# Experts' counts on TensorE: one load of 6 or 9 registers for two or three pairs, without assertions

## The chip, the cores and the metric

The kernel runs on one core of one Trainium2 chip. The metric is the device time of one execution in microseconds (us), the median of several runs.

## The reference

Two layers of a transformer over 256 latent tokens and 256 context tokens of width 1024. Each layer has a mixer (linear attention beside grouped attention in layer 0, a state-space scan beside Fourier mixing in layer 1) and a mixture of 16 experts. What the change touches is the experts:

```python
s = jax.nn.sigmoid((h @ router_w).astype(F32))
sel = (s + router_b).reshape(n, N_EXPERT_GROUPS, EXPERTS_PER_GROUP)
g_idx = jnp.argmax(lax.top_k(sel, TOP_K)[0].sum(-1), axis=-1)      # one group for each token
_, loc = lax.top_k(in_group, TOP_K)                                # two experts of it
...
return (jax.nn.silu(xb @ w_gate[ei]) * (xb @ w_up[ei])) @ w_down[ei]   # d_expert 768
```

Each token goes to two of the 16 experts and gets the weighted sum of their outputs. Layer 0 routes all 512 tokens, layer 1 the 256 latent ones. So each expert sees a number of tokens that is known at run time only: its count.

## The kernel before, in words

A program written with a planner: the source traces instructions in an order, and the planner orders each engine's queue by dependences, buffers and its own costs, unless an edge fixes it. Matrix products are fp32, with 32 tokens at a time in the array (128x32 weights load, 384 or 256 columns of expert weights streamed).

`experts` handles one layer. The 16 experts go in eight pairs (p, with m = 0 or 1 in it). For each pair `lists` builds from the routing positions which tokens go to it: VectorE writes a one-hot matrix `G` (tile G0p in layer 0, which has a single buffer), and TensorE multiplies it with a small table (`entries`, tile sl0p or sl1p, four matmuls for each half of a pair). In layer 0 the lists of pairs 0 and 1 are made ahead and in expert 0, and those of the last six pairs in one call, traced at the end of expert 1's iteration. GpSimd then gathers the pair's rows from DRAM (`gather`), TensorE transposes them (`features`, tile xt0p), `hidden` runs gate and up (tiles gu0p, gu1p; a part of 32 tokens at a time, over four weight chunks) and `down` the second product (dp0p, dp1p) one expert later. Results go back by a scatter (first pairs of layer 0) or by one-hot products (`combine`, cm0p, cm1p).

Parts of 32 tokens that may be empty stand in conditional blocks (`when`): TensorE compares a register with a constant and branches; where the expert has no such tokens, one short matmul with zeros fills the tile (the rows with `<-zero`). The registers come from `count(i)`: TensorE loads one number from the tile `cnt` (made on VectorE by `counts`: 16 counts, then 8 maxima of pairs, then one maximum over all) with an assertion that it is at most T. It is called for each expert (its count), for each pair at its first expert (the maximum) and for the next pair ahead of its transposes: 16 + 8 + 7 = 31 loads in a layer, all at line 1737. GpSimd and all engines together read a few more of `cnt` on their own lines.

The weights arrive by SyncE's queue, 1.5 MB a transfer (`wload`), into slots in a ring: a transfer waits until TensorE has read the slot's previous content.

While `self.pin` is set, `mm` and `tr` tie each matmul by `keep_in_program_order` behind the TensorE instruction traced just before it in the same block. Loads of registers and conditional blocks aren't tied themselves; they may be placed where their inputs are there, and a matmul traced behind a load is tied to that load and by nothing to the matmuls before it. `when` unsets `pin` inside its blocks.

Of the kernel before, what the change touches and what calls it, by code (L numbers as in the profile page):

```python
# [8 lines left out]
F32 = mybir.dt.float32  # L9
F32R = mybir.dt.float32r  # L10
BF16 = mybir.dt.bfloat16
I32 = mybir.dt.int32
U8 = mybir.dt.uint8
AF = mybir.ActivationFunctionType
OP = mybir.AluOpType
AX = mybir.AxisListType
# [8 lines left out]
T = 512  # L25
# [3 lines left out]
NE = 16  # L29
# [250 lines left out]
class Core:  # L280
# [63 lines left out]
    def mm(self, out, lhsT, rhs, start=True, stop=True):  # L344
        i = self.nc.tensor.matmul(out, lhsT, rhs, start=start, stop=stop, skip_group_check=True)  # L345
        if self.pin:
            self.tc.keep_in_program_order(i)

    def tr(self, out, x):
        i = self.nc.tensor.transpose(out, x, self.C('ident'))  # L350
# [1053 lines left out]
    def counts(self, l, count):  # L1404
        nc, pm, rp = self.nc, self.pm, self.rp
        NP = NE // 2
        cf = rp.tile([128, NE + NP + 1], F32, tag='r_cf', name=f'cf{l}')
        nc.vector.tensor_copy(cf[:, :NE], count)
        nc.vector.tensor_reduce(cf[:, NE:NE + NP], cf[:, :NE].rearrange('p (q m) -> p q m', m=2), axis=AX.X, op=OP.max)
        nc.vector.tensor_reduce(cf[:, NE + NP:], cf[:, :NE], axis=AX.X, op=OP.max)  # L1410
        cnt = pm.tile([128, NE + NP + 1], I32, tag='r_cnt', name=f'cnt{l}')
        nc.vector.tensor_copy(cnt, cf)

        wf = rp.tile([128, 2, NP], F32, tag='r_wf', name=f'wf{l}')
        nc.vector.tensor_scalar(wf[:, 0], cf[:, NE:NE + NP], 0.0, None, op0=OP.is_gt)
        for w in range(WIN[l], T >> l, WIN[l]):
            nc.vector.tensor_scalar(wf[:, 1], cf[:, NE:NE + NP], float(w), None, op0=OP.is_gt)
            nc.vector.tensor_tensor(wf[:, 0], wf[:, 0], wf[:, 1], op=OP.add)
        nwin = pm.tile([128, NP, 2], I32, tag='r_nw', name=f'nwin{l}')
        nc.vector.tensor_copy(nwin, wf[:, 0].unsqueeze(2).broadcast_to([128, NP, 2]))  # L1420
        nwin = nwin.rearrange('p q m -> p (q m)')
        return cnt, nwin
# [51 lines left out]
    def experts(self, l, nb, pm, rows, xg, zero, pos, number, aux):  # L1474
        nc, tc = self.nc, self.tc
        tn = nb * 128
        NP = NE // 2
# [5 lines left out]
        def when(rv, least, yes, no=None):  # L1483
            if rv is None:
                return yes()
            pin, self.pin = self.pin, False
            with tc.If(rv > least) as cmp:
                yes()
            if no:
                with cmp.Else():  # L1490
                    no()
            self.pin = pin

# [58 lines left out]

        def gather(idx, i, S, e=None):
            if S and e is not None:
                n = nc.gpsimd.value_load(cnt[0:1, e:e + 1], min_val=0, max_val=T)
                with tc.If(n > 64):
                    gather(idx, i, S)
                return  # L1560
            return nc.gpsimd.indirect_dma_start(out=xg[S], out_offset=None, in_=rows, bounds_check=tn - 1, oob_is_err=False,
                                         in_offset=bass.IndirectOffsetOnAxis(ap=idx[:, i, S:S + 1], axis=0))

        def features(nm, rv, xe, parts=(0, 1), G=None):
            for S in parts:
                x = self.spare('xe', S) if l else pm.tile([128, 1024], F32, tag=f'xe{S}', name=f'xe{l}{nm}{S}')
                x = x.rearrange('p (k s) -> p k s', k=KT)
                xe.append(x)
                p = [self.ps(f'xt{l}{nm}{S}{c}') for c in range(2)]

                def t_mm():
                    for k in range(KT):
                        if G:
                            for j in range(nb):
                                self.mm(p[k // 4][:, (k % 4) * 128:(k % 4 + 1) * 128], xg[j][:, k * 128:(k + 1) * 128], G[S][:, j],
                                        start=k % 4 == 0 and j == 0, stop=j == nb - 1)
                            continue
                        self.tr(p[k // 4][:, (k % 4) * 128:(k % 4 + 1) * 128], xg[S][:, k * 128:(k + 1) * 128])
                if S == 0:
                    t_mm()  # L1580
                else:
                    when(rv, 64, t_mm, lambda: [z_mm(p[c], 512) for c in range(2)])
                for c in range(2):
                    self.act(x[:, 4 * c:4 * c + 4], p[c].rearrange('p (k s) -> p k s', k=4), AF.Copy)
            return xe
# [9 lines left out]
        def scatter(Y, to, i, e):  # L1595
            def send(S):
                for q in range(4):
                    nc.gpsimd.indirect_dma_start(out=self.planes[q], out_offset=bass.IndirectOffsetOnAxis(ap=to[:, q, i, S:S + 1], axis=0),  # L1598
                                                 in_=Y[S][:, q // 2, (q % 2) * 256:(q % 2) * 256 + 256].bitcast(F32), in_offset=None,
                                                 bounds_check=2 * tn - 1, oob_is_err=False)  # L1600
            send(0)
            n = nc.gpsimd.value_load(cnt[0:1, e:e + 1], min_val=0, max_val=T)
            with tc.If(n > 64):
                send(1)

# [127 lines left out]
        def outputs(nm, n):  # L1733
            return [[pm.tile([128, 2, 512], F32R, tag=f'y{S}', bufs=2, name=f'y{l}{nm}{S}{h}') for h in range(n)] for S in range(2)]

        def count(i):
            return nc.tensor.value_load(cnt[0:1, i:i + 1], min_val=0, max_val=T)
        info = {}
        ns = 0 if l else NS

# [5 lines left out]

        def gathers(p):
            for S in range(2):
                gather(info[p][0][0], info[p][1], S, NE + p)
        xe, G0 = [], []  # L1750
        idx = some_lists(0, 1, lambda G: features('p0', None, xe, (0,), G))
        if l == 0:
            self.gate = gather(idx, 0, 0).ins
        cnt, nwin = self.counts(l, number)
        if l == 0:
            with tc.issue_after(self.gate):
                gather(idx, 0, 1, NE)

        nxt, last, Y, pend = xe if l else features('p0', None, xe, (0,)), None, None, None
        self.pin = True  # L1760
        for e in range(NE):
            p, m = divmod(e, 2)
            if m == 0:
                xe, ((idx, tok, gt, to), i) = nxt, info[p]
                ti = i - (NS - 2 if i else 0)
                full = count(NE + p)
                if 0 < p < NP - 1:
                    gathers(p + 1)
            rv = count(e)
            W = load_gu(e)  # L1770
            Wd = load_d(e - 1) if e else None

            def between():
                if e == 0:
                    features('p0', full, xe, (1,), G0)
                    some_lists(1, 1)
                    gathers(1)
                if m == 1 and pend:
                    combine(*pend)

            def middle():
                if last:
                    last[2] = transposed(*last[2])
            H = hidden(f'p{p}{m}', m, xe, gt, i, W, rv, middle, between)
            if m == 1 and p + 1 < NP:
                if l and p + 2 < NP:
                    some_lists(p + 2, 1)
                nxt = features(f'p{p + 1}', count(NE + p + 1), [])
            if m == 1:
                Y = outputs(f'p{p}', 1 + (p >= ns))  # L1790
            if last:
                down(*last[:3], Wd, last[3], Y)
            pend = None
            if m == 0 and e:
                if p > ns:
                    pend = (f'p{p - 1}', Y, *was[:3])
                else:
                    scatter([y[0] for y in Y], *was[3:])
                    if p == ns:
                        got = fetch(0)  # L1800
            if ns and 1 <= e - 2 * ns <= 2:
                collect(got, e - 2 * ns - 1)
                if e == 2 * ns + 1:
                    got = fetch(1)
            last, was = [f'p{p}{m}', m, (f'p{p}{m}', H), rv], (tok, ti, full, to, i, NE + p)
            if e == 1 and l == 0:
                some_lists(2, NP - 2)
        down(*last[:2], transposed(*last[2]), load_d(NE - 1), rv, Y)
# [4 lines left out]
            self.ada(1, 1, 'pj', pm.tile([128, 1024], F32, tag='xe0', name='adarow')[:, :512])  # L1813
            self.pin = pin

        most = nc.values_load(cnt[0:1, NE + NP:NE + NP + 1], min_val=0, max_val=T)
        with tc.If(most > WIN[l]):
            pw = pm.tile([128, nb, 2], F32, name=f'pw{l}')
            aw = pm.tile([128, nb, 2, NAUX[l]], F32 if l else F32R, name=f'aw{l}')
            with tc.For_i(0, NE, 2) as e:  # L1820
                nc.vector.tensor_copy(pw, pos[:, :, bass.ds(e, 2)])
                nc.vector.tensor_copy(aw, aux[:, :, bass.ds(e, 2), :].bitcast(F32))
                n = nc.values_load(nwin[0:1, bass.ds(e, 1)], min_val=0, max_val=4)
                with tc.For_i(1, n):
                    nc.vector.tensor_scalar(pw, pw, -1.0 * WIN[l], None, op0=OP.add)
                    idx, tok, gt, _ = lists('w', 1, 0, pw, aw, tail=1)
# [26 lines left out]
```

## Time and profile before

| | us |
|---|---|
| median of 3 runs (lowest, highest) | 1476.32 (1475.7, 1479.07) |
| profiled execution | 1479.13 |
| its span | 1477.4 |
| PE busy (share of the span) | 1250.3 (85%) |
| DVE busy | 682.2 (46%) |
| ACT busy | 398.0 (27%) |
| POOL busy | 140.8 (10%) |
| mean granted TensorE clock | 0.921 |

In the views PE is TensorE's matmuls, PEld its weight loads, PEq or PEldq its instruction sequencer, DVE VectorE, ACT ScalarE, POOL GpSimd, SP SyncE. A time is counted from the start of the span. An idle time stands in brackets with what ended it; "issue" is idle time in which the engine waited for nothing that the profile shows, that is, its sequencer had not got there. The experts of layer 0 take about 380 to 850 us of the span, those of layer 1 about 1100 to 1455. A granted clock of 1.00 is 2.4 GHz and 0.50 is 1.2 GHz.

### The profile page before, as it was taken

What the parts mean: (1) busy time and instruction counts of PE and PEld (TensorE: products, weight loads), DVE (VectorE), ACT (ScalarE), POOL (GpSimd) and SP (SyncE); (2) the same over time, 40 slices, a digit from 0 to 9 for tenths busy, and PEclk for the clock granted to TensorE, in tenths of its full rate; (3) what the DMA queues carried; (4) which work ended last, traced back from release to release, by engine and by line L of the source; (5) the groups of instructions that cost most, each with busy time, mean ns of one, the idle gap of its engine ahead of it and who ended that gap; (6) DMA issues with size and microseconds to landing.
All of it is one profiled execution on the core that took longest, in us unless ns stands there. A gap on an engine that the chain in (4) does not pass through costs nothing. (4 is left out here: it accounts for less than half of the span.)

```text
span 1477.4 us, 27647 instructions
## 1 busy us (share of the span) xinstructions
PE 1250.3 (85%) x11433; PEld 726.9 (49%) x11434; DVE 682.2 (46%) x1773; ACT 398.0 (27%) x791; POOL 140.8 (10%) x153
## 2 busy tenths in 40 slices
PE   4999988898679799999878867998978688898774
PEld 0697553576334344554434435876833344454333
DVE  1847536876425111111123568737665245454445
ACT  2624234344110110111010134434431112121214
POOL 0000011102101111022133012002010000000000
PEclk8999999899799999999989988999989898998996
DMA  9421688134488998889998341273388999999981
GB/s 359 163 100 43 223 323 343 52 128 161 178 338 315 382 412 369 347 329 421 426 386 341 144 160 55 89 278 150 129 340 360 377 412 425 423 426 421 425 367 31
DMA packets 49475, 411.87 MB, mean 279 GB/s; under 512 B 7195, under 2 KB 11439, under 8 KB 18064
## 3 DMA queue, kind: packets, MB, share of 16 engines
q1 hardware_dynamic: 41200, 388.40, 64.6%
q0 software_dynamic: 7232, 17.71, 3.3%
q8 instruction: 140, 2.29, 0.6%
q10 hardware_dynamic: 864, 3.15, 0.5%
q14 instruction: 39, 0.32, 0.1%
HBM read 402.02 MB, written 13.11 MB: 281 GB/s over the span
## 5 line engine op out<-in xcount | busy, mean ns | idle before, releaser
L1665 DVE SCALAR_TENSOR_TENSOR h0p<-gu0p,gt0p,sg0p 128x192 f32<-128x192 f32 x64 | 25.3, 415 | 177.0 <-ACT sg0p L321 176.5
L345 PE MATMUL gu0p<-big,xe0p 128*32 128x384 f32 x992 | 91.8, 492 | 1.6 <-issue 1.4
L345 PE MATMUL gu1p<-more,big 128*32 128x384 f32 x976 | 85.5, 493 | 7.9 <-issue 3.0
L321 ACT ACTIVATE sg0p<-gu0p 128x192 f32<-128x192 f32 x64 | 19.6, 331 | 247.1 <-PE gu0p L345 243.8
L345 PE MATMUL gu0p<-ring,xe0p 128*32 128x384 f32 x768 | 74.8, 497 | 0.8 <-ACT sg0p L321 0.5
L345 PE MATMUL gu0p<-more,xe0p 128*32 128x384 f32 x800 | 74.7, 493 | 0.5 <-issue 0.5
L345 PE MATMUL ada<-ring,small 128*32 128x512 f32 x344 | 62.9, 684 | 14.2 <-DMA ring<-in_ada 14.2
L1665 DVE SCALAR_TENSOR_TENSOR h1p<-gu1p,gt1p,sg1p 128x192 f32<-128x192 f32 x48 | 19.9, 415 | 118.0 <-ACT sg1p L321 117.9
L345 PE MATMUL dp0p<-big,hT0p 128*32 128x256 f32 x792 | 59.4, 402 | 6.3 <-issue 4.0
L345 PEld LDWEIGHTS gu1p<-more,big 128*32 128x32 f32 x976 | 35.1, 111 | 51.3 <-issue 46.1
L345 PEld LDWEIGHTS gu0p<-big,xe0p 128*32 128x32 f32 x992 | 37.8, 111 | 45.4 <-issue 42.1
L321 ACT ACTIVATE y0p<-dp0p 64x512 f32<-64x512 f32 (+1 forms) x40 | 23.6, 591 | 132.9 <-PE dp0p L345 105.0
L321 ACT ACTIVATE y1p<-dp1p 64x512 fp32r<-64x512 f32 x64 | 37.9, 592 | 79.9 <-PE dp1p L345 79.1
L321 ACT ACTIVATE sg1p<-gu1p 128x192 f32<-128x192 f32 x48 | 15.9, 330 | 156.4 <-PE gu1p L345 141.0
L321 ACT ACTIVATE big<-big 128x512 f32<-128x512 f32 (+2 forms) x81 | 44.7, 575 | 48.8 <-DVE big L641 21.5
L1598 POOL DMA_INDIRECT plane<-y0p,to0p x36 | 35.6, 988 | 205.8 <-ACT y0p L321 180.0
L345 PE MATMUL zo<-zo,zw 128*128 128x256 f32 x384 | 54.7, 292 | 0.0
L345 PE MATMUL gu1p<-big 128*32 128x384 f32 x528 | 52.5, 510 | 0.0
L345 PE MATMUL dp0p<-ring,hT0p 128*32 128x256 f32 x624 | 48.9, 401 | 3.5 <-issue 3.2
L345 PEld LDWEIGHTS zo<-zo,zw 128*128 128x128 f32 x384 | 48.6, 191 | 6.6 <-issue 4.3
L345 PEld LDWEIGHTS <-zero 128*128 128x128 bf16 x105 | 10.0, 97 | 83.2 <-issue 64.8
L1730 DVE TENSOR_TENSOR y1p<-dp1p,y1p 64x512 fp32r<-64x512 f32 x64 | 44.0, 688 | 5.5 <-ACT y1p L321 3.9
(558 smaller groups left out, 2425.2 us busy)
## 6 DMA issues: line engine op xcount, KB each, us to landing
more<-in_egu SPq DMA_DIRECT2D x54, 1536.0 KB, 15.3
big<-in_egu SPq DMA_DIRECT2D x48, 1536.0 KB, 15.6
ring<-in_ada SPq DMA_DIRECT2D x27, 1536.0 KB, 8.0
ring<-in_ed SPq DMA_DIRECT2D x27, 1536.0 KB, 14.8
ring<-in_egu SPq DMA_DIRECT2D x26, 1536.0 KB, 13.5
big<-in_ed SPq DMA_DIRECT2D x21, 1536.0 KB, 12.9
more<-in_ed SPq DMA_DIRECT2D x16, 1536.0 KB, 10.7
ring<-in_odw SPq DMA_DIRECT2D x5, 1536.0 KB, 6.2
```

The costliest lines, as they stand in the source:

```text
L321: a = self.nc.scalar.activation(out, x, func, **kw)
L345: i = self.nc.tensor.matmul(out, lhsT, rhs, start=start, stop=stop, skip_group_check=True)
L1598: nc.gpsimd.indirect_dma_start(out=self.planes[q], out_offset=bass.IndirectOffsetOnAxis(ap=to[:, q, i, S:S + 1], axis=0), in_=Y[S][:, q // ...
L1665: nc.vector.scalar_tensor_tensor(H[:, t], p[:, 192:384], gt[:, 2 * m + t % 2, i, t // 2:t // 2 + 1], sg, op0=OP.mult, op1=OP.mult)
L1730: nc.vector.tensor_tensor(yl[r, q], dp[r], yh[r, q].bitcast(F32), op=OP.subtract)
```

## The change

`counts` puts the numbers of a pair side by side: count, count, maximum, eight times, then the maximum over all. `some_counts(p, n)` loads those of n pairs into 3n registers of TensorE in one call without an assertion on the value; it is called for pairs 0 and 1 before the loop (6 registers), at expert 2 for pairs 2 to 4 and at expert 8 for pairs 5 to 7 (9 registers each). The two calls in the loop are queued behind the matmul traced last (`issue_after(self.last)`), which `mm` now notes and `when` restores. `count(i)` returns a register that is loaded. GpSimd's reads use the new places.

```diff
@@ -345,6 +345,7 @@
         i = self.nc.tensor.matmul(out, lhsT, rhs, start=start, stop=stop, skip_group_check=True)
         if self.pin:
             self.tc.keep_in_program_order(i)
+        self.last = i.ins
 
     def tr(self, out, x):
         i = self.nc.tensor.transpose(out, x, self.C('ident'))
@@ -1404,17 +1405,18 @@
     def counts(self, l, count):
         nc, pm, rp = self.nc, self.pm, self.rp
         NP = NE // 2
-        cf = rp.tile([128, NE + NP + 1], F32, tag='r_cf', name=f'cf{l}')
-        nc.vector.tensor_copy(cf[:, :NE], count)
-        nc.vector.tensor_reduce(cf[:, NE:NE + NP], cf[:, :NE].rearrange('p (q m) -> p q m', m=2), axis=AX.X, op=OP.max)
-        nc.vector.tensor_reduce(cf[:, NE + NP:], cf[:, :NE], axis=AX.X, op=OP.max)
-        cnt = pm.tile([128, NE + NP + 1], I32, tag='r_cnt', name=f'cnt{l}')
+        cf = rp.tile([128, 3 * NP + 1], F32, tag='r_cf', name=f'cf{l}')
+        c3 = cf[:, :3 * NP].rearrange('p (q x) -> p q x', x=3)
+        nc.vector.tensor_copy(c3[:, :, 0:2], count.rearrange('p (q m) -> p q m', m=2))
+        nc.vector.tensor_reduce(c3[:, :, 2], c3[:, :, 0:2], axis=AX.X, op=OP.max)
+        nc.vector.tensor_reduce(cf[:, 3 * NP:], c3[:, :, 2], axis=AX.X, op=OP.max)
+        cnt = pm.tile([128, 3 * NP + 1], I32, tag='r_cnt', name=f'cnt{l}')
         nc.vector.tensor_copy(cnt, cf)
...
@@ -1483,13 +1485,13 @@
         def when(rv, least, yes, no=None):
             if rv is None:
                 return yes()
-            pin, self.pin = self.pin, False
+            pin, self.pin, last = self.pin, False, self.last
             with tc.If(rv > least) as cmp:
                 yes()
             if no:
                 with cmp.Else():
                     no()
-            self.pin = pin
+            self.pin, self.last = pin, last
 
 
 
@@ -1554,7 +1556,7 @@
 
         def gather(idx, i, S, e=None):
             if S and e is not None:
-                n = nc.gpsimd.value_load(cnt[0:1, e:e + 1], min_val=0, max_val=T)
+                n = nc.gpsimd.value_load(cnt[0:1, 3 * e + 2:3 * e + 3], min_val=0, max_val=T)
                 with tc.If(n > 64):
                     gather(idx, i, S)
                 return
@@ -1733,8 +1735,16 @@
         def outputs(nm, n):
             return [[pm.tile([128, 2, 512], F32R, tag=f'y{S}', bufs=2, name=f'y{l}{nm}{S}{h}') for h in range(n)] for S in range(2)]
 
+
+        def some_counts(p, n):
+            _, v = nc.values_load_multi_w_load_instructions(cnt[0:1, 3 * p:3 * p + 3 * n], engines=[mybir.EngineType.PE], min_val=0, max_val=T,
+                                                            skip_runtime_bounds_check_because='counts of T tokens, compared with constants only')
+            for q in range(n):
+                regs[2 * (p + q)], regs[2 * (p + q) + 1], regs[NE + p + q] = v[3 * q:3 * q + 3]
+
         def count(i):
-            return nc.tensor.value_load(cnt[0:1, i:i + 1], min_val=0, max_val=T)
+            return regs[i]
+        regs = {}
         info = {}
         ns = 0 if l else NS
 
@@ -1746,7 +1756,7 @@
 
         def gathers(p):
             for S in range(2):
-                gather(info[p][0][0], info[p][1], S, NE + p)
+                gather(info[p][0][0], info[p][1], S, p)
         xe, G0 = [], []
         idx = some_lists(0, 1, lambda G: features('p0', None, xe, (0,), G))
         if l == 0:
@@ -1754,8 +1764,9 @@
         cnt, nwin = self.counts(l, number)
         if l == 0:
             with tc.issue_after(self.gate):
-                gather(idx, 0, 1, NE)
-
+                gather(idx, 0, 1, 0)
+
+        some_counts(0, 2)
         nxt, last, Y, pend = xe if l else features('p0', None, xe, (0,)), None, None, None
         self.pin = True
         for e in range(NE):
@@ -1766,6 +1777,9 @@
                 full = count(NE + p)
                 if 0 < p < NP - 1:
                     gathers(p + 1)
+            if e in (2, 8):
+                with tc.issue_after(self.last):
+                    some_counts(e // 2 + 1, 3)
             rv = count(e)
             W = load_gu(e)
             Wd = load_d(e - 1) if e else None
@@ -1802,7 +1816,7 @@
                 collect(got, e - 2 * ns - 1)
                 if e == 2 * ns + 1:
                     got = fetch(1)
-            last, was = [f'p{p}{m}', m, (f'p{p}{m}', H), rv], (tok, ti, full, to, i, NE + p)
+            last, was = [f'p{p}{m}', m, (f'p{p}{m}', H), rv], (tok, ti, full, to, i, p)
             if e == 1 and l == 0:
                 some_lists(2, NP - 2)
         down(*last[:2], transposed(*last[2]), load_d(NE - 1), rv, Y)
@@ -1813,7 +1827,7 @@
             self.ada(1, 1, 'pj', pm.tile([128, 1024], F32, tag='xe0', name='adarow')[:, :512])
             self.pin = pin
 
-        most = nc.values_load(cnt[0:1, NE + NP:NE + NP + 1], min_val=0, max_val=T)
+        most = nc.values_load(cnt[0:1, 3 * NP:3 * NP + 1], min_val=0, max_val=T)
         with tc.If(most > WIN[l]):
             pw = pm.tile([128, nb, 2], F32, name=f'pw{l}')
             aw = pm.tile([128, nb, 2, NAUX[l]], F32 if l else F32R, name=f'aw{l}')
```

## Rows read from the trace of the kernel before

**Rows 1.** View of one line, L1737, whole kernel: operation, count, ns min/median/max, starts.
```profile
L1737 PEldq TENSOR_LOAD <-cnt x62: 295/300/488, 382.7 to 1164.8; - x62
L1737 PEldq FUSED_REGOPS  x62: 146/146/160, 383.3 to 1165.2; - x62
```

**Rows 2.** The same view of L1737 in one burst of layer 1.
```profile
L1737 PEldq TENSOR_LOAD <-cnt x17: 295/300/312, 1140.9 to 1152.0; - x17
```

**Rows 3.** Timeline of PE, layer 1: start, us, line, tiles, count, idle before and releaser.
```profile
1140.81 2.78 PE L345 MATMUL gu1p<-big 128*32 128x384 f32 x30
1153.10 2.79 PE L345 MATMUL dp1p<-big,hT1p 128*32 128x256 f32 x24 [9.51 <-issue]
...
1164.76 9.24 PE L345 MATMUL gu1p<-more,big 128*32 128x384 f32 x112 [2.75 <-issue]
```

**Rows 4.** Windows, layer 0: length, PE, PEld, DVE, ACT, POOL busy, PEclk, DMA, GB/s.
```profile
620.00:660.00 40.00, 38.85 (x549) 19.99 (x542) 5.53 (x11) 5.56 (x14) 9.99 (x10) 1.00 0.82 334
```

**Rows 5.** Waits of SP's queue of transfers, 500 to 660 us: total, times, longest.
```profile
SPq L338 <- PE gu0p L345: 104.3, 14, 18.5
```

**Rows 6.** Windows, layer 1.
```profile
1340.00:1390.00 50.00, 38.75 (x374) 18.73 (x370) 23.50 (x77) 11.47 (x22) 0.99 (x1) 0.80 1.01 425
```

**Rows 7.** Windows of 4 us behind the bursts of layer 1.
```profile
1172.00:1176.00 4.00, 3.34 (x39) 1.82 (x30) 1.07 (x3) 0.66 (x2) 0.00 (x0) 1.00 0.36 152
1176.00:1180.00 4.00, 3.21 (x25) 2.74 (x25) 2.16 (x7) 1.08 (x3) 0.00 (x0) 1.00 0.68 243
1180.00:1184.00 4.00, 1.40 (x10) 0.49 (x13) 3.69 (x23) 1.64 (x3) 0.99 (x1) 0.91 1.04 442
1184.00:1188.00 4.00, 4.00 (x52) 1.89 (x48) 3.81 (x27) 0.00 (x0) 0.98 (x1) 0.66 0.99 418
```

**Rows 8.** Timeline of PE, start of layer 0's experts.
```profile
382.15 0.99 PE L345 MATMUL sl0p<-aux,G0p 128*128 128x10 f32 x4 [2.19 <-DVE cnt L1412]
...
391.32 1.94 PE L350 MATMUL xt0p<-const,xg 128*128 128x128 f32 x8 [5.99 <-DMA xg<-rows,idx0p]
...
411.73 0.61 PE L345 MATMUL sl0p<-aux,G0p 128*128 128x10 f32 x4
413.13 0.61 PE L345 MATMUL sl0p<-aux,G0p 128*128 128x10 f32 x4 [0.78 <-DVE G0p L1513]
```

**Rows 9.** Timeline of PE about the last loads of layer 0.
```profile
486.77 0.59 PE L345 MATMUL xt0p<-zero 128*128 128x512 bf16 x2 [1.46 <-ACT sg0p L321]
...
501.65 2.79 PE L345 MATMUL gu0p<-more,xe0p 128*32 128x384 f32 x32 [0.47 <-issue]
505.08 2.79 PE L345 MATMUL gu0p<-big,xe0p 128*32 128x384 f32 x32 [0.64 <-issue]
508.77 0.34 PE L345 MATMUL gu0p<-zero 128*128 128x384 bf16 x1 [0.90 <-issue]
511.07 0.50 PE L345 MATMUL gu0p<-zero 128*128 128x384 bf16 x1 [1.96 <-issue]
511.50 4.15 PE L345 MATMUL gu0p<-ring,xe0p 128*32 128x384 f32 x32
```

**Rows 10.** View of line L1487, its branches from 508.5 to 511.3 us.
```profile
L1487 PEldq COMPARE_BRANCH  x2: 215/1218/2220, 508.5 to 508.8; - x2
```

**Rows 11.** Timeline of PE at the lists of the last six pairs.
```profile
447.82 0.61 PE L345 MATMUL sl0p<-aux,G0p 128*128 128x10 f32 x4
...
451.62 1.50 PE L345 MATMUL gu0p<-more,xe0p 128*32 128x384 f32 x16
...
463.41 1.07 PE L345 MATMUL dp0p<-big,hT0p 128*32 128x256 f32 x16
...
469.05 0.61 PE L345 MATMUL sl0p<-aux,G0p 128*128 128x10 f32 x4
```

**Rows 12.** Timeline of DVE there.
```profile
451.73 0.69 DVE L1513 TENSOR_TENSOR G0p<-const,r_pos 128x512 fp32r<-128x512 f32 x1 [1.34 <-PE sl0p L345]
```

**Rows 13.** Timeline of PE at an odd expert of layer 0.
```profile
684.72 0.55 PE L350 MATMUL xt0p<-const,xg 128*128 128x128 f32 x3
```

More of the change, by code (lines that the diff above doesn't have):

```diff
@@ L1406, in counts @@
         NP = NE // 2
-        cf = rp.tile([128, NE + NP + 1], F32, tag='r_cf', name=f'cf{l}')
-        nc.vector.tensor_copy(cf[:, :NE], count)
-        nc.vector.tensor_reduce(cf[:, NE:NE + NP], cf[:, :NE].rearrange('p (q m) -> p q m', m=2), axis=AX.X, op=OP.max)
-        nc.vector.tensor_reduce(cf[:, NE + NP:], cf[:, :NE], axis=AX.X, op=OP.max)
-        cnt = pm.tile([128, NE + NP + 1], I32, tag='r_cnt', name=f'cnt{l}')
+        cf = rp.tile([128, 3 * NP + 1], F32, tag='r_cf', name=f'cf{l}')
[4 more added lines that the diff above has]
+        cnt = pm.tile([128, 3 * NP + 1], I32, tag='r_cnt', name=f'cnt{l}')
         nc.vector.tensor_copy(cnt, cf)
         wf = rp.tile([128, 2, NP], F32, tag='r_wf', name=f'wf{l}')
-        nc.vector.tensor_scalar(wf[:, 0], cf[:, NE:NE + NP], 0.0, None, op0=OP.is_gt)
+        nc.vector.tensor_scalar(wf[:, 0], c3[:, :, 2], 0.0, None, op0=OP.is_gt)
         for w in range(WIN[l], T >> l, WIN[l]):
-            nc.vector.tensor_scalar(wf[:, 1], cf[:, NE:NE + NP], float(w), None, op0=OP.is_gt)
+            nc.vector.tensor_scalar(wf[:, 1], c3[:, :, 2], float(w), None, op0=OP.is_gt)
             nc.vector.tensor_tensor(wf[:, 0], wf[:, 0], wf[:, 1], op=OP.add)
@@ L1601, in scatter @@
             send(0)
-            n = nc.gpsimd.value_load(cnt[0:1, e:e + 1], min_val=0, max_val=T)
+            n = nc.gpsimd.value_load(cnt[0:1, 3 * e + 2:3 * e + 3], min_val=0, max_val=T)
             with tc.If(n > 64):
```

## Prediction

> **What bounds the kernel now.** I read the profile in this order: the busy shares of the span in slices, the added code's line in the trace, the order of TensorE's work around that line, and then short windows of the two expert loops, to see which engine or queue sets their pace. The span is 1477.4 us, the execution took 1479.1 us with 1.7 us around the span, and the median of the runs shown is 1476.3 us, 2.8 us less.
>
> The line that reads a count ran 62 times, 31 in each layer: a TENSOR_LOAD of 0.300 us, a register operation of 0.146 us, and an assertion [rows 1]. In a burst they start 0.69 us apart (17 from 1140.9 to 1152.0 us [rows 2]), so 62 hold TensorE's sequencer for 43 us. This is not time of the multiplier: the sequencer runs ahead of it. How far is seen where that burst begins: matmuls that had been issued by then ran on from 1140.81 us for 2.78 us, so about 2.7 us of loading is covered, and what a burst has beyond that is seen as idle time "issue" [rows 3]. A reader has to sort the loads by this: alone or in pairs amid matmuls they cost nothing.
>
> The two loops have different limits. In layer 0 TensorE is busy 38.85 us of 40 while the DMA has slack (share 0.82) [rows 4], and the queue of weight transfers waits for slots that TensorE frees (104.3 us of 160 for one tile's matmuls alone [rows 5]); so what TensorE gains or loses before 660 us moves the whole rest. In layer 1 the DMA share is 1.01 with TensorE busy 38.75 us of 50 [rows 6]; there TensorE's time counts only where it leaves the DMA idle.
>
> **Loads removed, layer 1.** That burst stops TensorE for 9.51 us and a second one for 2.75 us [rows 3], 12.3 us in all. But the DMA lost its share only after them, 0.36 and 0.68 of 4 us each [rows 7], when too little was under way: 4 x (0.64 + 0.32) = 3.8 us of transfers. A stretch bound by transfers can get no more than that back from an earlier TensorE. I take 3.0 us, since slots freed earlier need not close both holes; the bounds are 0 and 3.8 us.
>
> **Loads removed, layer 0.** The first loads, from 382.7 us [rows 1], lie beside TensorE's wait for the gathered tokens (5.99 us, released by the DMA [rows 8]) and give nothing. The last, between 485 and 508 us, do cost: 1.46, 0.47, 0.64, 0.90 and 1.96 us idle, and 32 matmuls in 4.15 us after them where 32 like them take 2.79 [rows 9], 1.36 more. Sum 6.8 us. The 1.96 us contain a branch that took 2.22 us by itself [rows 10]; with 2.7 us queued it would be covered, so I count it. The bounds: 3.5 us (only the four shorter stops) and 6.8 us.
>
> **Loads added.** Six in the kernel, of 6 or 9 registers and without assertion. No row shows one. The lower bound is one TENSOR_LOAD, 0.3 us; the upper is n single ones, 6 x 0.69 = 4.1 and 9 x 0.69 = 6.2 us [rows 2]. I take 0.5 us, by the nearest row, a load that is one instruction; amid matmuls 2.7 us of queue hide it, and the first of layer 0 stands beside the wait for the gather. At the upper bound 6.2 - 2.7 = 3.5 us show at each of the two later loads of layer 0, 7.0 us together; in layer 1 the transfers cover them. The counts' new layout keeps the number of VectorE operations and GpSimd reads as often as before; nothing either way.
>
> By the Trainium skill ("Runtime: NRT & Kernel Launch", section "Instruction fetch mechanics") a register load costs about 200 ns per register even in bulk, which would be an estimate of 1.8 us for nine. The trace's single load took 0.300 us and no run here shows a multiple one; by that rule even nine registers vanish under the queue, and the third rival below goes, with its chance.
>
> **What moves: the order of TensorE's work.** This is what makes me cautious. Matmuls of the expert loop are kept in program order behind the TensorE instruction traced before them. A read of a count, itself free to move, cuts this chain before each expert, and the planner uses the cut: the last six pairs' lists (twelve groups of four matmuls, named sl0p, traced before expert 2) are spread through the gate-and-up work of expert 2 and the down work of expert 1. In the trace the twelve stand from 447.82 to 469.05 us with 16 such matmuls or so behind each, and TensorE doesn't idle [rows 11]. A group needs its one-hot matrix, which has one buffer and takes VectorE 0.69 us, after the group before [rows 12].
>
> After the change the load traced at expert 2 is queued behind the last matmul traced, which is the last of these twelve groups, and expert 2's gate-and-up is kept behind that load. So the groups can't be filled with it. Alone, a group comes every 1.40 us (411.73 to 413.13 us, 0.61 us long, 0.78 us idle behind it [rows 8]); eleven periods of 0.78 us idle leave 8.6 us empty that were full before. Expert 1's down matmuls may still move in, as they do in the trace at 463.41 us (16 in 1.07 us [rows 11]): one expert's first half is 48 matmuls in the code, two records each here, and these 96 fill six of the eleven gaps, and 5 x 0.78 = 3.9 us are left. The thin end can cost clock: behind a stretch in which TensorE was busy 1.40 of 4 us, the granted clock was 0.66 [rows 7], a stretch partly at 1.2 GHz. I add the 1.36 us that 32 matmuls lost so above, and a little for uneven filling: +5.5 us. The bounds are 0 (the planner keeps a mix) and 15 us: nothing fills and the clock is half, 0.99 us a group as at 382.15 us [rows 8] and 0.78 us for VectorE, so 12 x 0.99 + 11 x 0.78 = 20.5 us for what takes 12 x 0.61 = 7.3 us inside other work, and 1.4 us of slow matmuls behind it, 14.6.
>
> The token transposes for the next pair, which now stand inside the odd expert's gate-and-up (three of them take 0.55 us [rows 13]), lose their cut as well and go behind that expert's conditional parts. The down matmuls behind them cover the copy that follows; where they don't, each of six pairs could lose the 0.55 us twice. +1 us in layer 0, bounds 0 and 6.6 us. In layer 1 the transfers cover it.
>
> **Sum.** -3.0 - 6.8 + 5.5 + 1.0 = -3.3 us against the execution's own 1479.1, so 1475.8 us; against the median of the runs 1473.0 us. That this order effect takes back half of what the loads give is my forecast.
>
> **Rivals.**
> 1. No block: the planner finds other work for the gaps, or the chain is cut all the same. Then -3.0 - 6.8, with nothing lost, -9.8 us: 1466.5 us. For it: the trace shows an order with no idle time at that place [rows 11]. Against it: that order uses just the freedom that the edge removes.
> 2. Slower: the block stays bare. Its place is 447 to 470 us; the price is 15 us, and it decides from the point where the block costs more than the 9.8 us that the loads give. -9.8 + 15 + 1 = +6.2 us: 1482.5 us; at full clock it is -9.8 + 8.6 + 1, about nothing. For it: the down matmuls of expert 1 stand behind expert 2's gate-and-up in the trace's order [rows 11], and the clock has fallen behind thin work in this kernel [rows 7]. Against it: nothing in the code ties those matmuls to expert 2's gate-and-up; they need expert 1's hidden rows, which were done.
> 3. The load of several registers costs what single ones do. Then the forecast plus 7.0 us, +3.7: 1480.0 us. For it: so many registers are filled one after the other. Against it: the load itself is under half of the 0.69 us [rows 1], and the rest is not repeated.
> The Trainium skill ("TensorE: Matmul & The Clock Gate", section "A second HAM failure mode: psum-queue depth-cycling") says that short pauses repeated between groups of matmuls make the clock go up and down; that is rival 2's cold form, and 0.66 after 1.40 us busy of 4 agrees with it [rows 7].
>
> A further spread of some 3 us lies under all of them: taking out instructions shifts the branches, of which one took 0.215 us and the next 2.22 us [rows 10], and whether a long one meets an empty queue is chance.
>
> **How the numbers follow.** Forecast 0.42, rival 1 0.22, rival 2 0.28, rival 3 0.08. A measurement of this kernel tells about 0.2%, 3 us, from no change. The forecast at -3.3 with its spread is half on each side of that bound: faster 0.22, same 0.18, slower 0.02. Rival 1 adds 0.21 to faster and 0.01 to same; rival 2 0.01, 0.06 and 0.21; rival 3 0.03 to same and 0.05 to slower. Together 0.44, 0.28 and 0.28. The range runs from 1464 us (below rival 1 by its spread) to 1484 us (above rival 2); the forecast's own is 1468 to 1478.
>
> **What would show it.** Line 1737's loads gone and three multiple ones per layer in their place. No idle "issue" of 9.5 us near 1143 us, and the DMA share between 1172 and 1180 us near 1. In layer 0 the stops at 484 to 511 us gone. The twelve sl0p groups without gate-and-up matmuls between them, with down matmuls in half of the gaps, and VectorE's one-hot operation named as what ended the idle time. I am wrong if the groups are still mixed with expert 2's work, if they stand bare at half clock, if TensorE idles behind a multiple load, or if layer 1's end moves by much more than 4 us against layer 0's.

## The result and the profile after

The changed kernel takes 1485.26 us (median of 20 runs) against 1476.44 us: ratio 1.0065, interval 1.0051 to 1.0080, by the ratio 9.6 us slower. The forecast was 3 us faster, with a range to 1484 us. The profiled execution is a long one of its kernel, 1496.61 us (span 1494.5), so its stretches are read for what they hold, and sizes are taken from the ratios.

Timeline of TensorE in the changed kernel at the twelve list groups, which answers to [rows 11]:

```profile
444.02 6.96 PE L345 MATMUL dp0p<-big,hT0p 128*32 128x256 f32 x66 [5.02 <-issue]
450.91 0.61 PE L345 MATMUL sl0p<-aux,G0p 128*128 128x10 f32 x4
...
458.72 1.02 PE L345 MATMUL sl0p<-aux,G0p 128*128 128x10 f32 x4
...
465.29 1.94 PE L345 MATMUL dp0p<-ring,hT0p 128*32 128x256 f32 x16
...
474.93 1.02 PE L345 MATMUL sl0p<-aux,G0p 128*128 128x10 f32 x4 [0.78 <-DVE G0p L1515]
477.42 4.35 PE L345 MATMUL gu0p<-ring,xe0p 128*32 128x384 f32 x32 [1.47 <-issue]
```

No gate-and-up matmul stands between the groups any more; expert 1's down matmuls do, as forecast, in eight of the eleven gaps. But from the fifth group on a group takes 1.02 us in place of 0.61, and 16 down matmuls 1.94 in place of 1.07. Behind the block stand 1.47 us of "issue": the nine-register load, which ran from 474.93 us for 2.43 us. Windows of the same place (columns as in [rows 4]), and behind them one of the kernel before inside its twelve groups:

```profile
448.00:456.00 8.00, 7.20 (x72) 3.76 (x64) 3.51 (x5) 0.59 (x1) 0.00 (x0) 0.88 0.70 269
456.00:464.00 8.00, 7.77 (x61) 4.18 (x60) 2.31 (x4) 0.00 (x0) 0.00 (x0) 0.55 0.30 126
464.00:472.00 8.00, 7.30 (x43) 4.35 (x39) 2.77 (x4) 0.59 (x1) 1.59 (x2) 0.50 0.04 14
472.00:480.00 8.00, 4.96 (x30) 3.06 (x34) 5.84 (x31) 0.59 (x1) 6.06 (x7) 0.50 0.17 57
...
454.00:462.00 8.00, 8.00 (x88) 3.82 (x84) 3.07 (x6) 0.33 (x1) 0.00 (x0) 1.00 1.00 427
```

TensorE counts as nearly busy up to 472 us, at a granted clock of 0.50 (1.2 GHz). The transfers stop too (DMA share 0.04, where the kernel before has 1.00): of SyncE's queue, from 450 to 482 us, one transfer waits 30.4 us until expert 2's gate-and-up matmuls have read its slot:

```profile
SPq L338 <- PE gu0p L345: 30.4, 1, 30.4
```

One sign of the prediction did not come: the stops between 484 and 511 us were to be gone, but with no load near them there are stops of 1.46, 1.47 and 1.06 us at 506.47, 512.73 and 519.14 us. The first of them:

```profile
506.47 0.39 PE L345 MATMUL dp0p<-zero 128*128 128x512 bf16 x1 [1.46 <-issue]
```

In layer 1 the 9.51 us stop is gone; here is the place after the second load, and the windows that answer to [rows 7] and [rows 6]:

```profile
1155.27 2.22 PE L345 MATMUL gu1p<-ring,big 128*32 128x384 f32 x17 [2.43 <-issue]
```

```profile
1184.00:1188.00 4.00, 3.34 (x33) 2.58 (x26) 2.26 (x6) 0.99 (x3) 0.00 (x0) 1.00 1.01 424
...
1350.00:1400.00 50.00, 41.08 (x474) 21.05 (x464) 24.67 (x80) 12.47 (x25) 0.99 (x1) 0.93 1.01 424
```

The DMA has no hole in these windows; from the first list matmul of layer 1 to the first matmul of the last normalisation it took 355.0 us instead of 358.9. The loads themselves, by the view of their line:

```profile
L1740 PEldq TENSOR_LOAD <-cnt x6: 819/2182/2429, 395.7 to 1291.5; - x6
```

### The profile page after: what moved, and what is told of

It is laid out like the page before. It is cut to its first block, busy times and chain, and to the rows that moved or that the text cites. A ratio compares the mean times of both kernels' runs of the same rounds, so it can differ in the third digit from the quotient of the medians.

```text
span 1494.5 us, 27473 instructions
## 1 busy us (share of the span) xinstructions
PE 1251.7 (84%) x11433; PEld 750.5 (50%) x11434; DVE 682.8 (46%) x1773; ACT 398.2 (27%) x791; POOL 141.4 (9%) x153
## 5 line engine op out<-in xcount | busy, mean ns | idle before, releaser
L1667 DVE SCALAR_TENSOR_TENSOR h0p<-gu0p,gt0p,sg0p 128x192 f32<-128x192 f32 x64 | 25.2, 415 | 183.0 <-ACT sg0p L321 182.4
L345 PE MATMUL dp0p<-big,hT0p 128*32 128x256 f32 x792 | 63.2, 422 | 12.3 <-issue 5.3
L345 PEld LDWEIGHTS gu0p<-big,xe0p 128*32 128x32 f32 x992 | 41.7, 110 | 39.3 <-issue 31.0
L321 ACT ACTIVATE sg1p<-gu1p 128x192 f32<-128x192 f32 x48 | 15.8, 330 | 153.9 <-PE gu1p L345 138.0
L345 PEld LDWEIGHTS gu0p<-more,xe0p 128*32 128x32 f32 x800 | 31.5, 111 | 38.0 <-issue 31.1
L345 PEld LDWEIGHTS gu0p<-ring,xe0p 128*32 128x32 f32 x768 | 32.6, 112 | 34.2 <-issue 24.4
## 6 DMA issues: line engine op xcount, KB each, us to landing
big<-in_egu SPq DMA_DIRECT2D x48, 1536.0 KB, 17.2
```

Of the source, the lines that this page charges most:

```text
L321: a = self.nc.scalar.activation(out, x, func, **kw)
L1667: nc.vector.scalar_tensor_tensor(H[:, t], p[:, 192:384], gt[:, 2 * m + t % 2, i, t // 2:t // 2 + 1], sg, op0=OP.mult, op1=OP.mult)
```

## The experiments

My theory was A: the block of list groups costs the time. B: the nine-register loads and branches do. Times below are medians, with the ratio to the kernel before on the same chip; runs of different chips are compared by these ratios. Stretches are read from one execution of each kernel.

**One tie, taken away and put in.** e1_cut2 adds to the changed kernel, and e2_block to the kernel before:

```diff
+            if e == 2 and l == 0:
+                self.loose = True          # e1: the next pinned matmul gets no edge
...
+            if e == 2 and l == 0:
+                self.link = self.last      # e2: the next pinned matmul gets an edge to the last list group
```

Expected: 

> The changed kernel, with one edge less: expert 2's gate-and-up in layer 0 is not kept behind the new load, so it may fill the twelve list groups again. Theory A (the block of list groups, thin work at half clock, costs the time): about 10 us under the changed kernel's 1485 us, 1472 to 1478 us. Rival B (the nine-register loads, 2.2 to 2.4 us each, and branches that meet an empty queue cost it): no more than 2 us less, 1483 to 1487 us.

> The kernel before with its 62 single loads, and only expert 2's gate-and-up in layer 0 kept behind the last list group. A: 9 to 14 us over the kernel before, 1485 to 1491 us. B: as the kernel before, 1474 to 1479 us.

Measured: e1_cut2 1477.13 us, 1.0004 (0.9982 to 1.0027); e2_block 1489.3 us, 1.0066 (1.0046 to 1.0086). One edge is worth 9.0 us (1.0065 less 1.0004) out and 9.7 us in. The edge, and with it the block, is shown as a cause. But the loads' gain is missing: e1_cut2 has 3 loads a layer in place of 31 and is as slow as the kernel before.

**All the ties.** e3_cutall: new loads, `self.loose = self.pin` in `count`. e4_order: single loads, `self.link = self.last` in `count`.

Expected: 

> The changed kernel's loads with the order of the kernel before: the chain is cut at every place where a count was read. A: what the loads alone give, 3 to 10 us under the kernel before, 1467 to 1473 us. B: little changes against the changed kernel, 1482 to 1487 us. If the other lost cuts (token transposes of the next pair) cost something, it is below the kernel with the one cut at expert 2 by that much, 1 to 4 us.

> The kernel before with its 62 single loads, and every place tied where a read cut the chain: the new order alone. A: as with the one tie at expert 2 or up to 4 us more, 1485 to 1495 us. B: 1474 to 1479 us.

Measured: e4_order 1485.22 us, 1.0055 (1.0037 to 1.0072): the order alone makes the kernel slower, and the other ties add nothing to the one. e3_cutall 1484.9 us, 1.0044 (1.0027 to 1.0061), as B had it and not A: the old order with the new loads can't be told from the change. It is also 5.9 us above e1_cut2 (1.0044 less 1.0004), where the expectation had it 1 to 4 us below. Something else had to differ.

**The block's clock.** e6_fill adds three matmuls of zeros behind each group; e7_g2 gives the one-hot matrix two buffers:

```diff
+                        for _ in range(3 if n > 1 else 0):
+                            self.mm(p[:, 128:512], zero, zero.unsqueeze(1).broadcast_to([128, 3, 128]))
...
-                    ... tag='G', bufs=1, ...
+                    ... tag='G', bufs=2, ...
```

Expected: 

> The changed kernel as it is, with three short matmuls of zeros (384 columns, into columns that nobody reads) behind each of the twelve list groups. Theory A (most of the block's price is the half clock): the granted clock stays at 1.00 from 457 to 481 us, the block takes 17 to 20 us in place of 25, and the kernel gets 5 to 8 us faster for more work, 1477 to 1480 us. Rival B (the waits for the one-hot matrix and the order cost it): the added work is not paid back, 1485 to 1488 us.

> The changed kernel with two buffers for the one-hot matrix in layer 0, so a group need not wait for the one before it. Theory A: the twelve groups and the down matmuls stand closer, the block takes 14 to 18 us, the clock falls later or not: 4 to 8 us under the changed kernel, 1477 to 1481 us. Rival B (the block is not what costs): 1484 to 1487 us.

Windows and timeline of e6_fill at the block:

```profile
449.00:457.00 8.00, 8.00 (x66) 4.17 (x67) 3.57 (x6) 0.00 (x0) 0.00 (x0) 1.00 0.68 286
457.00:465.00 8.00, 8.00 (x79) 4.12 (x75) 3.30 (x6) 0.00 (x0) 0.00 (x0) 1.00 0.00 0
465.00:473.00 8.00, 3.99 (x22) 1.27 (x26) 6.14 (x55) 0.34 (x1) 1.00 (x1) 0.73 0.21 58
```

```profile
468.77 0.59 PE L345 MATMUL dp0p<-zero 128*128 128x512 bf16 x1 [2.15 <-DVE tg0p L1542]
471.07 5.44 PE L345 MATMUL gu0p<-ring,xe0p 128*32 128x384 f32 x29 [1.72 <-issue]
```

The clock stayed at 1.00 and the last group started 16.3 us after the first (465.49 less 449.19) instead of 24.0. Yet the kernel took 1487.3 us, 1.0066 (1.0044 to 1.0089). Behind the block stand a wait of 2.15 us for VectorE's lists, 1.72 us for the load and a slow clock (0.73). The half clock is seen, but that it carries the price isn't shown. What both have in common is that expert 2's gate-and-up, 128 records, comes after the block and not inside it, and that the transfers stand still in the block (share 0.00); yet neither trace has TensorE waiting for weights later in layer 0. And the 36 matmuls added, 72 instructions, move all the code behind them, which by what follows can be worth 7 us: the total of e6_fill decides nothing. e7_g2: 1483.47 us, 1.0045 (1.0023 to 1.0066), between its two ranges, 2.9 us less than the change at intervals that overlap.

**Where the loads stand.** e5_early is e1_cut2 with layer 0's three loads ahead of the first token transposes, each queued behind the one before. e8_sizes has loads of 1, 2, 3, 4, 6 and 8 registers there.

Expected: 

> The changed kernel with the cut at expert 2 (as e1_cut2), and in layer 0 all three loads (6, 9 and 9 registers) ahead of the first token transposes, beside TensorE's 7 us wait for the gather. Theory A (two nine-register loads stood behind a wait with nothing queued and showed 2.2 to 2.4 us each): 2 to 5 us under e1_cut2's 1477 us, 1472 to 1475 us. Rival B (branches and the placing of the collect step use up whatever is gained): 1476 to 1479 us.

> As e5_early, but layer 0's 24 registers come in six loads of 1, 2, 3, 4, 6 and 8, for the duration of each by its size. If a load costs a fixed price for each register, 0.14 us by six in 0.82 us: 0.14 to 1.1 us rising evenly. If it goes in blocks (six took 0.82 us, nine 2.2 us): 0.3 us for one, 0.8 for six and a jump at or before eight. The whole takes about as long as e5_early, 1472 to 1478 us.

Measured: e5_early 1472.67 us, 0.9981 (0.9958 to 1.0004), 3.4 us under e1_cut2 by the ratios, at intervals that overlap; A's direction. At the start of the sixth piece of 128 gate-and-up records it was 6.1 us ahead of the kernel before (107.7 us after the first transpose, against 113.8). That isn't the 6.8 us forecast for the loads: of the stops added up there only 1.46, 0.47 and 0.64 us, 2.57 together, lie ahead of this place, and the other stops of "issue" up to it differ by more, 9.6 us in the kernel before and 6.5 here. By the seventeenth piece it was 5.1 us behind (326.0 against 320.9). e8_sizes took 1475.84 us, a single run. Its loads of six (from number 10 of the tile) and of eight (from number 16), each in a view of its own moment:

```profile
L1780 PEldq TENSOR_LOAD <-cnt x1: 1477/1477/1477, 388.5 to 388.5; - x1
...
L1780 PEldq TENSOR_LOAD <-cnt x1: 607/607/607, 390.1 to 390.1; - x1
```

**What took the loads' gain back: the place of the code.** The timeline of e5_early in the stretch where it fell behind:

```profile
675.51 3.81 PE L347 MATMUL gu0p<-more,xe0p 128*32 128x384 f32 x25 [2.71 <-issue]
...
709.35 4.96 PE L347 MATMUL dp0p<-big,hT0p 128*32 128x256 f32 x59 [3.83 <-issue]
```

Both stops fall inside a row of like matmuls, and the sequencer shows no instruction in the first and one of 0.05 us at the start of the second. The trace's instruction queue has packets of 16,384 bytes; one started at 673.10 us, took 1.05 us and ended 1.36 us before TensorE went on, another started at 706.97, took 0.96 and ended 1.41 us before. The same distance stands ahead of other stops: 1.50 us at the 5.02 us stop of the changed kernel, 1.42 us at the 1.96 us stop of [rows 9], where TensorE was in a branch of 2.22 us. So I read these stops as TensorE waiting for its program, beside a DMA at 1.01; the profile doesn't name the wait. The Trainium skill ("Runtime: NRT & Kernel Launch", "Instruction fetch mechanics") says that the program comes in 16 KiB blocks of 256 instructions and that crossing one is mostly hidden; at these two places it wasn't. The change takes some 90 of TensorE's instructions out ahead of this place, so the blocks end elsewhere. Theory C: that is worth some us. Test: 42 tiny matmuls (84 instructions) at the start of the program, beside the wait for the first weights (10.0 us); 106 in e10_pad212, 64 ahead of the kernel before in e11_beforepad.

```diff
+            for _ in range(42):
+                nc.tensor.matmul(p[:32, :32], z, z, start=True, stop=True, skip_group_check=True)
             self.layer0()
```

Expected: 

> As e5_early, with 42 tiny matmuls of zeros (84 TensorE instructions) at the very start, beside the wait for the first weights. They put the experts' instructions of layer 0 back to the place that they have in the kernel before, counted from the program's start. Theory C (where the 16 KB instruction blocks end in the code, and so which branch or matmul waits for one, is worth some us): the stretch from the 12th to the 16th piece of 128 gate-and-up matmuls goes from 85.7 back to 78 to 80 us, idle issue there from 6.5 to about 3 us, and the kernel takes 1465 to 1469 us. Rival D (what is gained is lost to the transfers, wherever the code stands): 85 us there, and 1471 to 1475 us.

> As e9_pad84, with 106 tiny matmuls (212 instructions, half a 256-instruction block more). Theory C: the waits for instructions fall elsewhere, the time differs from e9_pad84 by some us, either way, 1466 to 1478 us. Rival D: as e5_early and e9_pad84 within 2 us.

> The kernel before with 64 tiny matmuls (128 instructions, half a block) at the start. Theory C: its time moves by 2 to 6 us, either way, though nothing else changes. Rival D: 1475 to 1478 us.

Measured: e9_pad84 1467.01 us, 0.9933 (0.9908 to 0.9958), 7.1 us under e5_early for 84 instructions more; the stretch fell from 85.7 to 79.9 us and "issue" in it from 6.5 to 2.8. e10_pad212 1468.58 us, 0.9947 (0.9925 to 0.9969), no different from e9_pad84: half a block isn't worse here, so "back to the old place" isn't the rule, only "another place"; its interval overlaps that of e5_early. e11_beforepad 1484.31 us, 1.0049 (1.0021 to 1.0077): the kernel before, moved by 128 instructions, loses 7.2 us, and its layer 1, from the first list matmul to the first of the last normalisation, takes 366.2 us in place of 358.9. That the place counts is shown, here and in the two pairs below; D is refuted. The padding's own work is not the reason: it makes one kernel faster and another slower, VectorE, ScalarE and GpSimd keep their order, and no matmul record stands more than six places from where it was. The reason, the wait for the program, is argued from the stops: those over 1 us that end 1.2 to 1.8 us behind such a packet sum to 17.2 us in layer 1 of the kernel before and 24.6 in e11_beforepad, and to 25.2 us in layer 0 of e5_early and 21.1 in e9_pad84.

**The change and e3_cutall with their code moved.** Both with the same 42 matmuls.

Expected: 

> The changed kernel as it is, with 42 tiny matmuls (84 instructions) at the start, which put layer 0's later experts back to the place in the code that they have in the kernel before. If part of the changed kernel's loss is the shifted code (C): 1477 to 1481 us, 4 to 8 under its 1485. If the block and the exposed loads are all of it: 1484 to 1487 us.

> As e3_cutall (the new loads with all the old cuts, 1485 us), with the same 84 instructions at the start. If its loss against the kernel before is the code's place (C): 1474 to 1479 us. If the added cuts or the exposed loads themselves cost it: 1483 to 1487 us.

Measured: e13_afterpad 1482.4 us, 1.0017 (1.0000 to 1.0033), between its two ranges; e14_cutpad 1474.33 us, 0.9960 (0.9943 to 0.9977). So of the change's 0.65%, 0.48 (7.1 us) go with the place of its code; the ties cost 0.57 (8.4 us, 1.0017 less 0.9960); and the new loads with the old order gain 0.40 (5.9 us). The three add up to the 9.6 us, as steps from one kernel to the next must. By the other way round, over e3_cutall, the place is worth 12.4 us (1.0044 less 0.9960) and the ties 3.1: so the shares depend on each other. Why e3_cutall gains 12.4 us by its padding stays open: its stops behind packets in layer 0 sum to 20.2 us, those of e14_cutpad to 18.7. That the ties cost 8 to 10 us is also what e1_cut2, e2_block and e4_order say. And the gain of 5.9 us is against a kernel before whose own place is worth 7.2 us.

In the profiles, one execution each and the change's a long one, part of the place's 7.1 us is seen in the block's clock. In e13_afterpad the same block stands in the same order, with this stop ahead of it and this window inside:

```profile
441.99 0.34 PE L345 MATMUL gu0p<-zero 128*128 128x384 bf16 x1 [1.73 <-issue]
...
456.00:464.00 8.00, 6.65 (x71) 4.09 (x59) 3.81 (x7) 0.64 (x2) 2.03 (x2) 0.93 0.12 45
```

The last group starts 18.5 us after the first (466.40 less 447.94) where the change takes 24.0. The granted clock fell to 0.50 only at 462.8 us, for 10.2 us; in the change, where the stop ahead is 5.02 us, it fell at 456.7 us, for 23.9 us. At the sixth piece e13_afterpad is 7.4 us ahead (120.5 us after the first transpose, against 127.9). So the ties' 8.4 us stand in a kernel whose profile has most of the block at full clock.

**Late collect, and a better version.** e12_late is e5_early with `collect` moved from the end of an expert into `between` of the next; e15_best is that with the 42 matmuls.

Expected: 

> As e5_early, with layer 0's collect step (transposes of the rows that GpSimd fetched back) traced half an expert later, so that TensorE need not stand 12 to 18 us waiting for them. If that wait is on the path: 1461 to 1467 us. If the transfers or what follows give the time back: 1470 to 1474 us.

> e9_pad84 with the collect step half an expert later, as in e12_late. If the two gains stand beside each other: 1462 to 1466 us. If the later collect only moves its wait: 1466 to 1469 us.

Measured: 1471.12 us, 0.9967 (0.9945 to 0.9989), and 1473.03 us, 0.9954 (0.9935 to 0.9972). TensorE's wait for GpSimd's rows fell from 12.8 us (e5_early) to 7.1 in e12_late, but is 17.3 in e15_best against 15.8 in e9_pad84, and nothing that these intervals tell is gained beyond e5_early, or beyond e9_pad84, which at 0.9933 beats both kernels; e15_best lies above both of its ranges.

**Eight at a time.** e16_eights is e14_cutpad with loads `cnt[0:1, a:a + 8]` for a = 0, 8, 16.

Expected: 

> As e14_cutpad, but the three loads of a layer have 8 registers each and start at numbers 0, 8 and 16 of the tile, at the same places of the program (before the loop, at experts 2 and 8). If where a load starts decides its price (eight from number 16 took 0.61 us in e8_sizes, six from number 10 took 1.48, nine from 6 or 15 take 2.2): about 0.6 us for each of the six, the idle time behind the two in layer 0 down by some 3 us, and the kernel 1 to 4 us under e14_cutpad. If the number of registers decides: about 2 us each and no change.

```profile
L1749 PEldq TENSOR_LOAD <-cnt x6: 592/598/780, 395.7 to 1301.2; - x6
```

Six loads of about 0.60 us, the first of layer 0 0.78: eight from 0, 8 or 16 are cheaper than six or nine from other starts. The start alone doesn't decide, for six from 0 took 0.82 us in layer 1 where eight from 0 took 0.59. The stops behind the two later loads of layer 0 fell from 2.39 us each in e14_cutpad to 0.79 and 0.87, as expected, but the kernel took 1473.17 us, 0.9954 (0.9934 to 0.9974), which can't be told from e14_cutpad.

## Why the prediction was wrong

In the sum's own terms: the loads, taken out and put in, were put at -9.8 us and gave -5.9; the order at +6.5 and cost 8.4; the place of the code at nothing and cost 7.1. From -3.3 us that is 3.9, 1.9 and 7.1 us more, the 9.6 measured (along the one way of splitting it over e13_afterpad and e14_cutpad).

- **"Loads removed, layer 1", -3.0 us:** right in kind and size in the profiles (358.9 to 355.0 us; 355.7 in e13_afterpad, 354.4 in e14_cutpad), though single executions stray: 358.8 in e5_early with the new loads, 355.5 in e4_order with the single ones.
- **"Loads removed, layer 0", -6.8 us:** too large. It counted the 1.96 us stop behind a 2.22 us branch as the price of loads, but that stop ended 1.42 us behind a packet of the instruction queue, like the stops of 1.46, 1.47 and 1.06 us that the changed kernel has at 506 to 519 us without loads. How much of the 6.8 us was the loads' no run shows alone.
- **"Loads added", hidden by 2.7 us of queue:** wrong twice. A nine-register load takes 2.2 to 2.4 us, not 0.5, and where it stands little is queued: at expert 2 of layer 0 `issue_after` puts it behind list groups that wait for VectorE one by one, in layer 1 behind a single matmul of zeros (0.39 us). So 1.47 and 0.92 us showed in layer 0, 2.43 and 2.44 in layer 1. Moving layer 0's ahead gave back 3.4 us, at intervals that overlap. By the Trainium skill ("Runtime: NRT & Kernel Launch", "Instruction fetch mechanics"), whose 200 ns a register is for loads from HBM, the estimate for nine was 1.8 us. That is near the 2.2 us here, from an on-chip tile, but far from the 0.60 us for eight from number 8 or 16. The error was the cover.
- **"The order of TensorE's work", +5.5 and +1 us:** the mechanism was right, filler included; the size was 8.1 to 9.7 us in four comparisons (3.1 in the one over e3_cutall). The clock term, put at 1.36 us for 32 matmuls, was mis-sized for the change: the granted clock was 0.50 for 23.9 us. How the price divides between clock and order stays open after e6_fill; that e13_afterpad pays 8.4 us with 10.2 us at half clock speaks for the order.
- **The largest step, the place of the code:** "A further spread of some 3 us ... is chance". The prediction saw that taking out instructions shifts the branches, but put the shift at nothing in the sum. It wasn't chance from run to run but belongs to each program, 7.1 us here, against a kernel before that stood in the better of the two places tried (1476 and 1484 us). Without it the change is at 1.0017, and with -3.3 forecast against +2.5 us measured it would still have been missed, by the loads and the order.
- **Rivals:** 2 (slower, 1482.5 us) came nearest, and its half clock came, once and for 23.9 us; but the block was filled, not bare, and 7.1 us of the loss have another cause. 3 was half right: TensorE did stop behind the loads, but nine registers took 2.2 us and not 6.2.

## What to carry to other kernels

Removing instructions moves all the code behind them; where a program is long, branches and shares a busy DMA, compare a change at two or three places of its code before its gain or loss is believed. A load tied "behind the last matmul" is covered only if that matmul doesn't itself wait and enough work stands queued with it. And an instruction that nobody minds may be what lets a planner mix two kinds of work: look at what stood between the neighbours before taking it out.

## What the runs showed of the hardware

A register load from the count tile took 0.30 us for one (single loads of the kernel before) and 0.60 us for eight from 0, 8 or 16; six from 0 took 0.82 us, and the first load of layer 0 some 0.2 us more (0.78 for eight, 1.02 for six). From starts that aren't a multiple of eight it was about 0.25 us for each register (three 0.77, four 1.00, six 1.48, each seen once; nine 2.2 us). Moving a program by 128 instructions, with no other change, cost 7.2 us of 1477.
